# Token-block order for the last two column blocks of a residual projection, and router bookkeeping moved into the first expert pair, in a mixed attention and mixture-of-experts block on one Trainium2 core

## The chip, the cores and the metric

The kernel runs on 1 core of one Trainium2 chip. The metric is the device time in microseconds (us) from the start to the end of one execution. Lower is better. The engines are called PE (matrix multiply), DVE (vector), ACT (scalar activation), POOL (GpSimd) and SP (the queue that issues most DMA transfers).

## What is computed

One layer for 512 tokens of width 1024, all in 32-bit floating point: a merged recurrent and forgetting-attention part, a cross attention over 256 memory rows, and then a mixture of 32 experts of which each token takes two. The change lies between the last product of the cross attention and the first two experts:

```python
x = x + _cross_attention(...)              # its last step is  o @ w_xo,  w_xo is 1024 x 1024
t = _rmsnorm(x, g_moe)
g_logits = t @ w_rg + b_rg                 # 4 groups
e_logits = t @ w_re + b_re                 # 4 groups of 8 experts
g_idx = argmax(g_logits); top_v, top_i = top_k(e_logits of that group, 2)
top_w = softmax(top_v) * softmax(g_logits)[g_idx]
for e in range(32):
    he = silu(t @ w_gate[e]) * (t @ w_up[e])
    y = y + combine[:, e:e + 1] * (he @ w_down[e])
return _rmsnorm(x + y, g_final)
```

The three matrices of one expert are 2 MB each, 201 MB for all 32.

## The kernel before

**The last projection.** `o @ w_xo` is added to the residual `X1` in four column blocks of 256 columns (c = 0 to 3). The 512 tokens are four token blocks (tb = 0 to 3). A weight block of 512 rows x 256 columns (0.5 MB, tile `wraw`) is loaded on SP by `load_w`, split by ACT into a high part `wh` (L124) and by DVE into the rest `wl` (L125), and used by `Rows.block`: four slices of the contraction, three matmuls each (L102 to L104), so 12 matmuls for one token block and half the contraction. Three `wraw` buffers are used in turn, and a new load waits until the block three before it has been split. Blocks c = 2 and 3 are `rw2` and `rw3`.

**The router.** For each token block the new residual rows are transposed on PE (`turn`, L765, copied out by ACT or DVE as `rsc`), multiplied with the router's weights (`logits`, L780), squared on ACT (`squares`, `rstd`, with a power on POOL), scaled into two half-precision parts `xn16` (`parts`: L797 on ACT, L798 on DVE), and for each pair of token blocks h the two experts are chosen on DVE (`choose`), every token gets a rank within its expert (`place`, a few small matmuls L843), and one-hot matrices `G0` are made. `first` (L896) then gathers on PE the tokens of experts 0 and 1 with 64 matmuls. `numbers` makes the slot-to-token table and what later pairs need (`code`, `R`, `tokf`), and `weights` the weight of each slot (`wsl`).

**The order.** In this section PE, DVE and ACT run exactly in the order in which the program writes their steps, and the string `ROUT` sets it: `a`, `b` are halves of `rw2` by token block, `e` adds `rw2` to the residual, `w` is a token block of `rw3`, `v` splits the second weight block of `rw3`, `t`, `l`, `s`, `r`, `X`, `g` are the router's steps above, `C` chooses, `K` places, `G` gathers. SP and POOL are ordered by the scheduler of the compiler.

**The experts.** They run in 16 pairs. A pair has 16 steps of gate and up matmuls (`gate_up`, L1053), 8 steps of down matmuls of the pair before (L1077), two gathers for the next pair (`stationary`, L1028), and the combination of the pair before into the residual (L1103, L1104). Weights come in pieces of 1 MB, 12 in a pair, through a ring of 14 pieces that `RING` lays out: `m` pieces in a pool, `h` and `l` in the buffers of `wh` and `wl`, `r` in space that is free after the projection. `experts.load(9)` issues the first nine `m` pieces before the router starts.

Of the kernel before, what the change touches and what calls it, by code (L numbers as in the profile page):

```python
# [9 lines left out]
F32 = mybir.dt.float32  # L10
F32R = mybir.dt.float32r
# [9 lines left out]
P = 128  # L21
# [15 lines left out]
CAP = 64  # L37
NPAIR = NE // 2
MAXOV = 16
NRAW = 10  # L40
RING = "m m m m m m m m m h l r r m".split()
NAHEAD = 11


ROUT = ("a0 a1 t00 a2 t01 l00 a3 t02 l01 b0 t03 l02 v b1 l03 b2 b3 e s0 s1 w0 t10 t11 s2 w1 l10 l11 t12 t13 s3 r0 w2 l12 "
        "l13 r1 t20 X0 w3 r2 t21 l20 g0 X1 r3 t22 l21 g1 C0 t23 l22 l23 K0 g2 g3 C1 X2 K1 X3 G0 G1")
NR = 8 + NE

C_MLQ, C_MLK, C_MLV, C_MLO = 0, 512, 1024, 2048
# [8 lines left out]
def emit(ctx, tc, a):  # L58
# [51 lines left out]
    def load_w(src, k0, nk, c0, n):  # L110
        i = wx[0] if wx else -1
        if wx:
            wx[0] += 1
        pool, nb = (wx[1], 3) if i == 0 else (wp, 3)
        raw = pool.tile([P, 1024], F32, name="wraw", tag="wraw", bufs=nb)
        SP.dma_start(raw.rearrange("p (j n) -> p j n", j=nk),
                     src[k0 * P:(k0 + nk) * P, c0:c0 + n].rearrange("(j p) n -> p j n", p=P))
        if i == 2:
            h = wx[1].tile([P, 1024], F32R, name="wh", tag="wraw", bufs=3)
            l = wx[1].tile([P, 1024], F32R, name="wl", tag="wraw", bufs=3)  # L120
        else:
# [537 lines left out]

    mraw = ctx.enter_context(right("mraw"))  # L660
    wx[:] = [0, s_ot.enter_context(left("wx"))]
    router, experts = moe(ctx, tc, a, X1, dram, small, acc, pss, pso, left, right, ident, rpow, wp, rt_, mraw)
    rw2, rw3 = (resid_rows(a["w_xo"], oth, otl, c) for c in (2, 3))
    with tc.manual_schedule(engines={mybir.EngineType.PE, mybir.EngineType.DVE, mybir.EngineType.Activation}):
        rw2.loads()
        rw3.ws = [rw3.load(0)]
        experts.load(9)
        for w in ROUT.split():
            n = [int(x) for x in w[1:]]
            if w[0] in "ab":  # L670
                drain(rw2.block(4 * "ab".index(w[0]), rw2.ws["ab".index(w[0])], n[0]))
            elif w == "e":
                rw2.done()
            elif w == "v":
                rw3.ws.append(rw3.load(4))
                experts.load(NAHEAD)
            elif w[0] == "w":
                drain(rw3.of_block(n[0]))
            else:
                router[w[0]](*n)  # L680
    s_ot.close()
# [44 lines left out]
    return c  # L726


def moe(ctx, tc, a, X2, dram, small, acc, pss, pso, left, right, ident, rpow, wp, c, mraw):
    nc = tc.nc  # L730
    V, S, G, TE, SP = nc.vector, nc.scalar, nc.gpsimd, nc.tensor, nc.sync
    rc, iot, Eb, Ab, rk, tokf, wsl = c.pool, c.iot, c.Eb, c.Ab, c.rk, c.tokf, c.wsl
# [8 lines left out]

    c.hits = hits

    slots, tTs = [], []

    sq, lgs, m8s, ids = {}, {}, {}, {}
    ss = rc.tile([P, NB, 2], F32, name="ss")

    READY = ((0, 4), (4, 6), (6, 8))

    def turned(stage, tb):

        if not tTs:
            tTs.append(mraw.tile([P, 4, 4, P], F32, name="rsc", tag="mw", bufs=NRAW))
        k0, k1 = READY[stage]
        if stage == 0:
            return tTs[0][:, tb]
        return tTs[0][:, 2 * stage - 2 + tb // 2, tb % 2 * 2:tb % 2 * 2 + 2]

    def turn(stage, tb):  # L760
        k0, k1 = READY[stage]
        n = k1 - k0
        pt = pss()
        for j in range(n):
            TE.transpose(pt[:, j * P:(j + 1) * P], X2[tb][:, (k0 + j) * P:(k0 + j + 1) * P], ident)  # L765
        ptv = pt[:, :n * P].rearrange("p (j t) -> p j t", j=n)
        if stage == 2:
            V.tensor_copy(turned(stage, tb), ptv)
        else:
            S.activation(turned(stage, tb), ptv, AF.Copy)  # L770

    lp = []

    def logits(stage, tb):

        if not lp:
            lp.append(pso())
        k0, k1 = READY[stage]
        for k in range(k0, k1):
            TE.matmul(lp[0][:, tb * NR:(tb + 1) * NR], turned(stage, tb)[:, k - k0], c.wr[:, k],  # L780
                      start=k == 0 and tb == 0, stop=k == KB - 1 and tb == NB - 1, skip_group_check=True)

    def squares(tb, cs=slice(0, 6 * P), i=0):
        S.activation(c.XN[:, 0, tb, cs].bitcast(BF), X2[tb][:, cs], AF.Square, accum_out=ss[:, tb, i:i + 1])

    def rstd(tb):
        squares(tb, slice(6 * P, D), 1)
        v = small.tile([P, 1], F32, name="vv", tag="vv")
        V.tensor_scalar(v, ss[:, tb, 0:1], ss[:, tb, 1:2], D * EPS, op0=OP.add, op1=OP.add)
        V.tensor_scalar(v, v, 1.0 / (D * XS * XS), None, op0=OP.mult)  # L790
        sq[tb] = rpow(v)
# [62 lines left out]
        for tb in (2 * h, 2 * h + 1):  # L854
            hits(c.G0, c.GA, cd[:, tb % 2], tb)

    def numbers(h):

        bs = slice(2 * h, 2 * h + 2)

        jk = rc.tile([P, 2, 2, NE], F32, name="jk", tag="jk", bufs=1)
        rf = small.tile([P, 2, 2], F32, name="rf", tag="rf")
        V.tensor_scalar(rf, rk[:, bs], -FAR, None, op0=OP.add)
        V.tensor_mul(jk, Eb[:, bs], rf[:, :, :, None].to_broadcast([P, 2, 2, NE]))
        V.scalar_tensor_tensor(c.code[:, bs], jk[:, :, 0], FAR, jk[:, :, 1], op0=OP.add, op1=OP.add)
# [22 lines left out]
    def first(h):  # L888

        if not c.pts:  # L890
            c.pts += [pss(), pss()]
        for g, pt in enumerate(c.pts):
            for i in range(4):
                for j in range(4):
                    tb, k = 2 * h + i // 2, 4 * g + j
                    TE.matmul(pt[:, j * P:(j + 1) * P], c.XN[:, i % 2, tb, k * P:(k + 1) * P], c.G0[:, tb],  # L896
                              start=h + i + j == 0, stop=h == 1 and i + j == 6, skip_group_check=True)

    router = dict(G=first, X=parts, C=choose, K=place, t=turn, l=logits, s=squares, r=rstd, g=scaled)
    c.numbers = numbers  # L900
    experts = Experts(ctx, tc, a, X2, dram, small, acc, pss, pso, left, right, ident, rpow, wp, c, mraw)
    return router, experts

# [1 line left out]
class Experts:  # L905
# [29 lines left out]
    def piece(self, src, w, h, kind):  # L935

        r, n = ((4, DE), (4, DE), (2, D))[w]
        src = src[:, h * r:(h + 1) * r]
        if kind in "mr":
            pool, nb = (self.mraw, NRAW) if kind == "m" else (self.mr2, 2)  # L940
# [25 lines left out]
def run_experts(ex, ctx, tc, a, X2, dram, small, acc, pss, pso, left, right, ident, rpow, wp, c, mraw):  # L966
# [5 lines left out]
    gfin = sg.tile([P, D], F32, name="gfin")  # L972
    G.dma_start(gfin, a["g_final"].to_broadcast([P, D]))

    def weights():

        wpt = c.wparts
        dn = sg.tile([P, NB], F32, name="dn")
# [6 lines left out]
        V.tensor_copy(wpt[:, :, :, 1], rem)  # L985
        V.tensor_sub(rem, rem, wpt[:, :, :, 1])
        V.tensor_copy(wpt[:, :, :, 2], rem)
        pw = pss()
        for tb in range(NB):
            for j in range(2):  # L990
                Vw = sg.tile([P, 3, NE], BF, name="Vw", tag="Vw", bufs=1)
                V.tensor_mul(Vw, Eb[:, tb, j][:, None, :].to_broadcast([P, 3, NE]),
                             wpt[:, tb, j, :, None].to_broadcast([P, 3, NE]))
                TE.matmul(pw[:, :3 * NE], c.R[:, tb, j], Vw.rearrange("p a e -> p (a e)"),
                          start=tb + j == 0, stop=tb + j == NB)
        pwv = pw[:, :3 * NE].rearrange("p (v a b) -> p v a b", v=3, b=2)
        for h in range(2):
            r = slice(h * 64, h * 64 + 64)
# [290 lines left out]
```

## Time and profile before

| | |
|---|---|
| median of 3 runs | 1309.62 us (1306.95 to 1310.33) |
| the profiled execution | 1310.08 us, its span 1308.3 us |
| PE busy | 1253.9 us, 96% of the span |
| DVE, ACT, POOL busy | 42%, 27%, 10% |
| moved by DMA | 278.45 MB, mean 213 GB/s |
| chain that ended last | PE 92%, DVE 4%, ACT 1% |

Times in the trace are counted from the span's start. The projections before the section of the change end near 748 us, the router runs to 806 us, and the sixteen expert pairs follow.

### The profile page before, as it was taken

How to read it: one execution, taken by the hardware profiler on the slowest of the kernel's cores; microseconds unless marked ns; L12 is line 12 of the kernel's file. 1: busy time of each engine (PE TensorE's matmuls, PEld its weight loads, DVE VectorE, ACT ScalarE, POOL GpSimd, SP SyncE). 2: the span in 40 equal slices, each digit the busy share in tenths (PEclk: the TensorE clock that was granted, in tenths of full speed). 3: DMA queues.
4: the chain of work that ended last, by engine and by line, in shares of the span. 5: the costliest groups of instructions: out<-in, count | busy, mean ns of one | idle time of the engine just before them, and what ended most of it. 6: DMA issues, size and time to landing. Idle time of an engine off the chain costs nothing.

```text
span 1308.3 us, 18639 instructions
## 1 busy us (share of the span) xinstructions
PE 1253.9 (96%) x7606; PEld 899.9 (69%) x7606; DVE 552.9 (42%) x1054; ACT 355.4 (27%) x627; POOL 130.0 (10%) x250
## 2 busy tenths in 40 slices
PE   6999999999999999999999985999999999999996
PEld 5898999888888977899977983444444444444443
DVE  4436455334566654447555435132323322222225
ACT  4435344222344433235434351000000000000102
POOL 0001011000001010001000003111111211111001
PEclk9999999999999999999999996899999999999998
DMA  4342432344254325234521553999999999999971
GB/s 166 86 109 84 79 95 72 92 97 92 86 89 81 89 87 155 91 119 138 186 70 62 209 211 124 361 409 417 417 416 416 419 417 416 414 418 417 418 324 66
DMA packets 99113, 278.45 MB, mean 213 GB/s; under 512 B 6196, under 2 KB 67908, under 8 KB 77904
## 3 DMA queue, kind: packets, MB, share of 16 engines
q1 hardware_dynamic: 97536, 272.46, 58.1%
q0 software_dynamic: 1488, 4.76, 1.1%
q8 instruction: 61, 1.00, 0.3%
q14 instruction: 28, 0.23, 0.1%
HBM read 275.08 MB, written 2.12 MB: 212 GB/s over the span
## 4 chain that ended last, share of the span: by engine, by line
PE 92%; DVE 4%; ACT 1%; issue 1%; DMA 1%; POOL 0%; SPq 0%; POOLq 0%; ACTq 0%; DVEq 0%
PE acc L1053 18%; PE acc L102 16%; PE acc L104 16%; PE acc L103 16%; PE pso L1077 8%; PE pss L1028 4%; PE pss L1103 1%; PE pso L1103 1%; PE pso L1104 1%; PE pss L102 1%; PE pss L104 1%; PE pss L103 1%; PE pss L1066 1%; PE pss L1104 1%; DVE st L1030 1%
## 5 line engine op out<-in xcount | busy, mean ns | idle before, releaser
L1053 PE MATMUL acc<-mw,st 128*64 128x512 f32 x880 | 239.5, 608 | 0.0
L125 DVE TENSOR_TENSOR wl<-wraw,wh 128x1024 fp32r<-128x1024 f32 x120 | 146.9, 1225 | 193.0 <-ACT wh L124 188.5
L124 ACT ACTIVATE wh<-wraw 128x1024 fp32r<-128x1024 f32 x120 | 126.9, 1059 | 195.2 <-PE acc L103 92.5
L1053 PEld LDWEIGHTS acc<-mw,st 128*64 128x64 f32 x880 | 68.1, 139 | 111.1 <-issue 106.9
L102 PE MATMUL acc<-hH,wh 128*128 128x512 f32 x320 | 128.5, 401 | 0.0
L103 PE MATMUL acc<-hL,wh 128*128 128x512 f32 x320 | 127.7, 399 | 0.0
L104 PE MATMUL acc<-hH,wl 128*128 128x512 f32 x320 | 125.9, 401 | 1.7 <-DVE wl L125 1.7
L1088 DVE SCALAR_TENSOR_TENSOR yl<-pso,wsl,yh 128x512 fp32r<-128x512 f32 x32 | 22.6, 747 | 225.4 <-ACT yh L1087 225.4
L1077 PE MATMUL pso<-mw,hT 128*64 128x512 f32 x440 | 112.6, 592 | 0.7 <-ACT hT L1068 0.7
L103 PE MATMUL acc<-wl,hH 128*128 128x256 f32 x384 | 109.3, 285 | 1.1 <-DVE wl L125 1.1
L102 PE MATMUL acc<-wh,hH 128*128 128x256 f32 x384 | 109.4, 286 | 0.8 <-ACT wh L124 0.8
L104 PE MATMUL acc<-wh,hL 128*128 128x256 f32 x384 | 109.1, 285 | 0.2 <-DVE hL L196 0.2
L1039 POOL TENSOR_SCALAR G<-iot,code 128x64 f16<-128x64 f32 x120 | 50.7, 449 | 342.5 <-PE pss L1028 322.9
L1077 PEld LDWEIGHTS pso<-mw,hT 128*64 128x64 f32 x440 | 37.2, 137 | 61.4 <-issue 59.7
L103 PEld LDWEIGHTS acc<-wl,hH 128*128 128x128 f32 x384 | 73.1, 191 | 1.9 <-DVE wl L125 1.5
L102 PEld LDWEIGHTS acc<-wh,hH 128*128 128x128 f32 x384 | 72.8, 190 | 1.7 <-ACT wh L124 1.2
L104 PEld LDWEIGHTS acc<-wh,hL 128*128 128x128 f32 x384 | 73.3, 191 | 0.5 <-DVE hL L196 0.4
L104 PEld LDWEIGHTS acc<-hH,wl 128*128 128x128 f32 x320 | 60.6, 189 | 16.0 <-DVE wl L125 2.2
L1028 PEld LDWEIGHTS <-xn 128*128 128x128 f16 x960 | 55.3, 99 | 23.2 <-issue 22.7
L103 PEld LDWEIGHTS acc<-hL,wh 128*128 128x128 f32 x320 | 60.7, 190 | 13.4
L102 PEld LDWEIGHTS acc<-hH,wh 128*128 128x128 f32 x320 | 60.6, 189 | 13.3 <-ACT wh L124 0.4
L1087 ACT ACTIVATE yh<-pso,wsl 128x512 fp32r<-128x512 f32 x32 | 20.3, 684 | 154.1 <-PE pso L1077 154.1
(321 smaller groups left out, 2341.0 us busy)
## 6 DMA issues: line engine op xcount, KB each, us to landing
mw<-w_gate SPq DMA_DIRECT2D x55, 1024.0 KB, 12.7
mw<-w_up SPq DMA_DIRECT2D x55, 1024.0 KB, 11.7
mw<-w_down SPq DMA_DIRECT2D x55, 1024.0 KB, 10.1
wraw<-w_in SPq DMA_DIRECT2D x64, 512.0 KB, 5.5
wraw<-w_xkv SPq DMA_DIRECT2D x16, 512.0 KB, 3.4
mwl<-w_gate SPq DMA_DIRECT2D x10, 512.0 KB, 8.7
mwh<-w_up SPq DMA_DIRECT2D x10, 512.0 KB, 8.9
mwh<-w_down SPq DMA_DIRECT2D x10, 512.0 KB, 11.1
```

The source lines that it names most:

```text
L102: TE.matmul(out, ah, bh, start=start, stop=False, **kw)
L103: TE.matmul(out, ah, bl, start=False, stop=False, **kw)
L104: TE.matmul(out, al, bh, start=False, stop=stop, **kw)
L124: S.activation(h, raw, AF.Copy)
L125: V.tensor_sub(l, raw, h.bitcast(F32))
L1028: TE.matmul(pt[:, j * n:(j + 1) * n], c.XN[:, i % 2, i // 2, (4 * g + j) * P:(4 * g + j + 1) * P], G_[:, i // 2, :n], start=i == 0, stop=i ...
L1039: G.tensor_scalar(G_[:, tb, i * 64:i * 64 + 64], iot[:, :64], c.code[:, tb, e:e + 1], None, op0=OP.is_equal)
L1053: TE.matmul(ps[i][half(h)], sts[k // 4][:, k % 4, half(h)], w[i][k], start=k == 0, stop=k == KB - 1)
L1077: TE.matmul(o[n][half(h)], hT[:, j, half(h)], w[j][:, n * 512:(n + 1) * 512], start=j == 0, stop=j == 3)
L1088: V.scalar_tensor_tensor(yl[:k, c], o[n][:k], wcol, yh[:k, c].bitcast(F32), op0=OP.mult, op1=OP.subtract)
L1103: TE.matmul(o, C[:k, ts], yh[:k, c], start=True, stop=False)
L1104: TE.matmul(o, C[:k, ts], yl[:k, c], start=False, stop=True)
```

## The change

Both `rw2` and `rw3` are now done whole by token block (`x` and `p` in `ROUT`), each token block is added to the residual at once, and the router's steps of token blocks 0 and 1 come between. The transposes have two stages of 512 columns in place of three of 512, 256 and 256. The split parts of the two weight blocks of `rw2` have buffers of their own, while all four `wraw` blocks share the three common buffers. `v` comes first. The slot numbers and weights are taken out of the stretch ahead of the first pair and put behind its sixth step. The ring still has 14 pieces, with nine `m` and three `r`.

```diff
-NRAW = 10
-RING = "m m m m m m m m m h l r r m".split()
+NRAW = 9
+NTAIL = 3
+RING = "m m m m m m m m m h l r r r".split()
-ROUT = ("a0 a1 t00 a2 t01 l00 a3 t02 l01 b0 t03 l02 v b1 l03 b2 b3 e s0 s1 w0 t10 t11 s2 w1 l10 l11 t12 t13 s3 r0 w2 l12 "
-        "l13 r1 t20 X0 w3 r2 t21 l20 g0 X1 r3 t22 l21 g1 C0 t23 l22 l23 K0 g2 g3 C1 X2 K1 X3 G0 G1")
+ROUT = ("v x0 t00 t01 s0 l00 p0 t02 l01 t03 s1 r0 x1 l02 t10 X0 l03 p1 l10 r1 s2 x2 t11 X1 s3 g0 l11 g1 C0 p2 r2 x3 t12 "
+        "X2 K0 l12 g2 p3 t13 r3 l13 g3 C1 G0 K1 X3 G1")
...
-        pool, nb = (wx[1], 3) if i == 0 else (wp, 3)
-        raw = pool.tile([P, 1024], F32, name="wraw", tag="wraw", bufs=nb)
+        raw = wp.tile([P, 1024], F32, name="wraw", tag="wraw", bufs=3)
...
-        if i == 2:
-            h = wx[1].tile([P, 1024], F32R, name="wh", tag="wraw", bufs=3)
-            l = wx[1].tile([P, 1024], F32R, name="wl", tag="wraw", bufs=3)
+        if i in (0, 1):
+            h = wx[1].tile([P, 1024], F32R, name="wh", tag="wx", bufs=4)
+            l = wx[1].tile([P, 1024], F32R, name="wl", tag="wx", bufs=4)
...
-            if w[0] in "ab":
-                drain(rw2.block(4 * "ab".index(w[0]), rw2.ws["ab".index(w[0])], n[0]))
-            elif w == "e":
-                rw2.done()
-            elif w == "v":
+            if w == "v":
                 rw3.ws.append(rw3.load(4))
                 experts.load(NAHEAD)
-            elif w[0] == "w":
-                drain(rw3.of_block(n[0]))
+            elif w[0] in "xp":
+                drain((rw2 if w[0] == "x" else rw3).of_block(n[0]))
...
-    READY = ((0, 4), (4, 6), (6, 8))
+    READY = ((0, 4), (4, 8))
...
-    def numbers(h):
+    def codes(h):
...
+    def numbers(h):
...
         if not c.pts:
             c.pts += [pss(), pss()]
-        for g, pt in enumerate(c.pts):
-            for i in range(4):
+        for i in range(4):
+            for g, pt in enumerate(c.pts):
...
-    def weights():
+    Vw = sg.tile([P, 2 * NB, 3, NE], BF, name="Vw")
+
+    def weight_parts():
...
+        V.tensor_mul(Vw, Eb.rearrange("p b j e -> p (b j) e")[:, :, None, :].to_broadcast([P, 2 * NB, 3, NE]),
+                     wpt.rearrange("p b j a -> p (b j) a")[:, :, :, None].to_broadcast([P, 2 * NB, 3, NE]))
+
+    def weights():
+
         pw = pss()
-        for tb in range(NB):
-            for j in range(2):
-                Vw = sg.tile([P, 3, NE], BF, name="Vw", tag="Vw", bufs=1)
-                V.tensor_mul(Vw, Eb[:, tb, j][:, None, :].to_broadcast([P, 3, NE]),
-                             wpt[:, tb, j, :, None].to_broadcast([P, 3, NE]))
-                TE.matmul(pw[:, :3 * NE], c.R[:, tb, j], Vw.rearrange("p a e -> p (a e)"),
-                          start=tb + j == 0, stop=tb + j == NB)
+        for i in range(2 * NB):
+            TE.matmul(pw[:, :3 * NE], c.R[:, i // 2, i % 2], Vw[:, i].rearrange("p a e -> p (a e)"),
+                      start=i == 0, stop=i == 2 * NB - 1)
...
-            for h in range(2):
-                c.numbers(h)
...
+            if p == 0:
+                advance(gu, 6)
+                with tc.manual_schedule(engines={mybir.EngineType.DVE, mybir.EngineType.Activation}):
+                    for f in (c.codes, c.numbers):
+                        for h in range(2):
+                            f(h)
+                    weight_parts()
...
-            advance(gu, 4)
+            advance(gu, 4 if p else 2)
...
-            advance(gu, 4)
+            advance(gu, 4 if p else 0)
```

**On SP, at the end of the projection.** `wraw` are weight blocks of `w_xo`, `mw` the first nine pieces of expert weights, `mwl` the first piece that goes into the buffers of `wl`. Before:

```order
L116 DMA wraw_7209<-w_xo 128x4x256
L116 DMA wraw_7215<-w_xo 128x4x256
L116 DMA wraw_7337<-w_xo 128x4x256
L942 DMA mw_7221<-w_gate 128x2048
L942 DMA mw_7223<-w_up 128x2048
L942 DMA mw_7225<-w_gate 128x2048
L942 DMA mw_7227<-w_up 128x2048
L942 DMA mw_7229<-w_up 128x2048
L942 DMA mw_7231<-w_gate 128x2048
L942 DMA mw_7233<-w_up 128x2048
L942 DMA mw_7235<-w_gate 128x2048
L942 DMA mw_7237<-w_gate 128x2048
```

And now:

```order
L116 DMA wraw_7215<-w_xo 128x4x256
L931 DMA mw_7221<-w_gate 128x2048
L931 DMA mw_7223<-w_up 128x2048
L931 DMA mw_7225<-w_gate 128x2048
L931 DMA mw_7227<-w_up 128x2048
L931 DMA mw_7229<-w_up 128x2048
L931 DMA mw_7231<-w_gate 128x2048
L931 DMA mw_7233<-w_up 128x2048
L931 DMA mw_7235<-w_gate 128x2048
L931 DMA mw_7237<-w_gate 128x2048
L116 DMA wraw_7239<-w_xo 128x4x256
L936 DMA mwl_7249<-w_gate 128x1024
```

The second weight block of `rw3` (7337 before, 7239 now) has moved from ahead of the nine pieces to behind them. The first block of `rw2` (7203) has moved too: before it was issued during the `w_xkv` loads, now it stands three places ahead of the pieces.

**On ACT, at the same place.** `wh` are the high parts of the weight blocks, `rsc` the transposed residual, `xn16,ss` the squares. Before:

```order
L124 ACTIVATE wh_7205<-wraw_7203 128x1024
L124 ACTIVATE wh_7211<-wraw_7209 128x1024
L124 ACTIVATE wh_7217<-wraw_7215 128x1024
L770 ACTIVATE rsc_7268<-pss_7263 128x512
L770 ACTIVATE rsc_7268<-pss_7282 128x512
L770 ACTIVATE rsc_7268<-pss_7305 128x512
L770 ACTIVATE rsc_7268<-pss_7327 128x512
L124 ACTIVATE wh_7339<-wraw_7337 128x1024
```

And now:

```order
L124 ACTIVATE wh_7205<-wraw_7203 128x1024
L124 ACTIVATE wh_7211<-wraw_7209 128x1024
L124 ACTIVATE wh_7217<-wraw_7215 128x1024
L124 ACTIVATE wh_7241<-wraw_7239 128x1024
L757 ACTIVATE rsc_7283<-pss_7278 128x512
L757 ACTIVATE rsc_7290<-pss_7285 128x512
L770 ACTIVATE xn16_7195,ss_7196<-x1_4532 128x512
L757 ACTIVATE rsc_7328<-pss_7323 128x512
```

The split of the second weight block of `rw3` now stands ahead of the first copy of a transpose. On DVE its other half (`wl_7242`) stands in the same way ahead of the first addition of `rw2` to the residual.

**On DVE, at the end of the router.** `GA` and `G0` are the one-hot matrices that `first` needs, `code`, `R` and `Vj` belong to the slot numbers, `st` is the scaled gather with which the first pair starts. These rows follow the ranks of the second pair of token blocks now:

```order
L849 TENSOR_TENSOR jk_8184<-eb_5658,rf_8185 128x128
L734 TENSOR_SCALAR GA_5667<-iot_5647,cd_7688 128x128
L850 SCALAR_TENSOR_TENSOR code_5665<-jk_8184 128x64
L856 TENSOR_TENSOR R_5661<-iot64_5649,rk_5660 128x512
L862 TENSOR_SCALAR Vj_8189<-eb_5658,tokn_5651 128x64
L735 SCALAR_TENSOR_TENSOR G0_5666<-iot_5647,cd_7688,GA_5667 128x128
L734 TENSOR_SCALAR GA_5667<-iot_5647,cd_7688 128x128
L862 TENSOR_SCALAR Vj_8189<-eb_5658,tokn_5651 128x64
L856 TENSOR_TENSOR R_5661<-iot64_5649,rk_5660 128x512
L735 SCALAR_TENSOR_TENSOR G0_5666<-iot_5647,cd_7688,GA_5667 128x128
L784 SCALAR_TENSOR_TENSOR xn16_7195<-x1_4532,rpow_7613,xn16_7195 128x1024
L1022 TENSOR_TENSOR st_8158<-pss_7643,gsc_5640 128x512
```

Though the program writes them behind the sixth step of the first pair, `code`, `R` and half of `Vj` stand on DVE still ahead of `st`, between the one-hot matrices. Only the other half of `Vj`, `tokf` and the weights come after `st`.

## Rows read from the trace of the kernel before

**Rows 1.** Busy time by stretch: length, PE, PEld, DVE, ACT, POOL, granted clock, DMA share, GB/s.
```profile
750.00:800.00 50.00, 37.51 (x325) 36.17 (x324) 26.55 (x95) 22.69 (x47) 2.79 (x5) 0.86 0.56 211
1000.00:1100.00 100.00, 99.22 (x606) 45.01 (x604) 29.52 (x46) 8.13 (x14) 14.58 (x27) 1.00 1.01 417
```

**Rows 2.** Timeline of PE: the same instruction in two successive expert pairs (start, duration).
```profile
867.50 0.75 PE L1066 MATMUL pss<-ident,ul 128*128 128x128 f32 x4
897.68 0.75 PE L1066 MATMUL pss<-ident,ul 128*128 128x128 f32 x4
```

**Rows 3.** Timeline of PE: end of the router and the first expert pair.
```profile
794.28 0.18 PE L843 MATMUL pso<-ab,before 128*128 128x32 bf16 x1 [5.34 <-DVE ab L834]
...
806.25 13.43 PE L1053 MATMUL acc<-mw,st 128*64 128x512 f32 x48
...
823.59 3.61 PE L1028 MATMUL pss<-G,xn 128*128 128x128 f16 x32
827.13 4.66 PE L1053 MATMUL acc<-mw,st 128*64 128x512 f32 x16
...
833.62 0.64 PE L1053 MATMUL acc<-mw,st 128*64 128x512 f32 x1
```

**Rows 4.** Busy time by 2 us stretches (columns as in rows 1).
```profile
806.00:808.00 2.00, 2.00 (x8) 0.73 (x9) 0.40 (x3) 0.00 (x0) 2.00 (x6) 0.50 0.04 8
...
812.00:814.00 2.00, 2.00 (x12) 0.63 (x10) 0.00 (x0) 0.00 (x0) 2.00 (x2) 0.97 0.24 45
...
824.00:826.00 2.00, 2.00 (x22) 2.00 (x20) 0.85 (x5) 0.00 (x0) 0.00 (x0) 0.50 1.01 422
```

**Rows 5.** SP's timeline; time to landing of issues at 736.01, 736.98, 739.90, and of all.
```profile
736.98 0.42 SPq L942 DMA_DIRECT2D mw<-w_up  x1
...
739.90 2.57 SPq L942 DMA_DIRECT2D mw<-w_gate  x2
...
wraw<-w_xo SPq DMA_DIRECT2D x1, 512.0 KB, 3.4
mw<-w_up SPq DMA_DIRECT2D x1, 1024.0 KB, 7.6
mw<-w_gate SPq DMA_DIRECT2D x1, 1024.0 KB, 21.1
...
mw<-w_gate SPq DMA_DIRECT2D x55, 1024.0 KB, 12.7
```

**Rows 6.** Timelines of PE, ACT, DVE: 24 projection matmuls from 747.84, transposes, logits, copy, splits.
```profile
747.84 0.28 PE L102 MATMUL acc<-wh,oth 128*128 128x256 f32 x1
...
750.66 0.60 PE L765 MATMUL pss<-ident,x 128*128 128x128 f32 x4
...
752.96 0.98 PE L780 MATMUL pso<-wr,rsc 128*128 128x40 f32 x8
...
751.29 0.60 ACT L770 ACTIVATE rsc<-pss 128x512 f32<-128x512 f32 x1 [1.24 <-PE pss L765]
...
759.15 1.05 ACT L124 ACTIVATE wh<-wraw 128x1024 fp32r<-128x1024 f32 x1
...
760.24 1.23 DVE L125 TENSOR_TENSOR wl<-wraw,wh 128x1024 fp32r<-128x1024 f32 x1 [8.74 <-ACT wh L124]
```

**Rows 7.** Timelines of ACT and DVE: `parts`, and first and last step of `choose` and `place`.
```profile
781.25 2.15 ACT L797 ACTIVATE xn<-x,rpow 128x1024 f16<-128x1024 f32 x1 [0.52 <-POOL rpow L98]
...
783.71 0.29 DVE L813 MAX8 m<-lg 128x8 f32<-128x8 f32 x2
...
786.61 0.19 DVE L834 TENSOR_TENSOR ab<-eb 128x64 bf16<-128x64 bf16 x1
788.38 0.29 DVE L846 TENSOR_TENSOR jk<-eb,pso 128x128 f32<-128x128 bf16 x1 [1.25 <-PE pso L843]
...
790.53 0.35 DVE L739 SCALAR_TENSOR_TENSOR G<-iot,cd,GA 128x128 f16<-128x128 f32 x1
...
798.60 2.05 DVE L798 SCALAR_TENSOR_TENSOR xn<-x,rpow,xn 128x1024 f16<-128x1024 f32 x1
```

More of the change, by code (lines that the diff above doesn't have):

```diff
@@ L661, in emit @@
     wx[:] = [0, s_ot.enter_context(left("wx"))]
-    router, experts = moe(ctx, tc, a, X1, dram, small, acc, pss, pso, left, right, ident, rpow, wp, rt_, mraw)
+    router, experts = moe(ctx, tc, a, X1, dram, small, acc, pss, pso, left, right, ident, rpow, wp, rt_, mraw, wx[1])
     rw2, rw3 = (resid_rows(a["w_xo"], oth, otl, c) for c in (2, 3))
@@ L726, in router_consts, with moe @@
     return c
-def moe(ctx, tc, a, X2, dram, small, acc, pss, pso, left, right, ident, rpow, wp, c, mraw):
+def moe(ctx, tc, a, X2, dram, small, acc, pss, pso, left, right, ident, rpow, wp, c, mraw, wx):
     nc = tc.nc
@@ L742, in moe @@
     c.hits = hits
-    slots, tTs = [], []
+    slots, tTs = [], {}
     sq, lgs, m8s, ids = {}, {}, {}, {}
     ss = rc.tile([P, NB, 2], F32, name="ss")
-    READY = ((0, 4), (4, 6), (6, 8))
[L751 to L758, printed above, removed]
+    READY = ((0, 4), (4, 8))
     def turn(stage, tb):
-        k0, k1 = READY[stage]
-        n = k1 - k0
         pt = pss()
[L764 to L768, printed above, removed]
+        for j, k in enumerate(range(*READY[stage])):
+            TE.transpose(pt[:, j * P:(j + 1) * P], X2[tb][:, k * P:(k + 1) * P], ident)
+        t = tTs[stage, tb] = wx.tile([P, 4, P], F32, name="rsc", tag="rsc", bufs=2)
+        ptv = pt.rearrange("p (j t) -> p j t", j=4)
+        if (stage, tb) == (1, NB - 1):
+            V.tensor_copy(t, ptv)
         else:
-            S.activation(turned(stage, tb), ptv, AF.Copy)
+            S.activation(t, ptv, AF.Copy)
     lp = []
@@ L777, in logits, with squares @@
             lp.append(pso())
-        k0, k1 = READY[stage]
-        for k in range(k0, k1):
-            TE.matmul(lp[0][:, tb * NR:(tb + 1) * NR], turned(stage, tb)[:, k - k0], c.wr[:, k],
+        for j, k in enumerate(range(*READY[stage])):
+            TE.matmul(lp[0][:, tb * NR:(tb + 1) * NR], tTs[stage, tb][:, j], c.wr[:, k],
                       start=k == 0 and tb == 0, stop=k == KB - 1 and tb == NB - 1, skip_group_check=True)
-    def squares(tb, cs=slice(0, 6 * P), i=0):
+    def squares(tb, cs=slice(0, D // 2), i=0):
         S.activation(c.XN[:, 0, tb, cs].bitcast(BF), X2[tb][:, cs], AF.Square, accum_out=ss[:, tb, i:i + 1])
     def rstd(tb):
-        squares(tb, slice(6 * P, D), 1)
+        squares(tb, slice(D // 2, D), 1)
         v = small.tile([P, 1], F32, name="vv", tag="vv")
@@ L865, in numbers @@
         V.scalar_tensor_tensor(c.code[:, bs], jk[:, :, 0], FAR, jk[:, :, 1], op0=OP.add, op1=OP.add)
+    def numbers(h):
+        bs = slice(2 * h, 2 * h + 2)
         Vj = rc.tile([P, 2, 2, NE], F16, name="Vj", tag="Vj", bufs=1)
@@ L899, in moe @@
     router = dict(G=first, X=parts, C=choose, K=place, t=turn, l=logits, s=squares, r=rstd, g=scaled)
-    c.numbers = numbers
+    c.codes, c.numbers = codes, numbers
     experts = Experts(ctx, tc, a, X2, dram, small, acc, pss, pso, left, right, ident, rpow, wp, c, mraw)
@@ L939, in piece @@
         if kind in "mr":
-            pool, nb = (self.mraw, NRAW) if kind == "m" else (self.mr2, 2)
+            pool, nb = (self.mraw, NRAW) if kind == "m" else (self.mr2, NTAIL)
             t = pool.tile([P, r, n], F32, name="mw", tag="mw", bufs=nb)
```

## The prediction, made before the changed kernel was run

> **What bounds the kernel now.** I read the stretches first, then PE's timeline, then who it waits for, then the transfers. In the expert pairs PE is busy 99.22 of 100 us and the DMA engines are full at 417 GB/s [rows 1]. One pair takes 897.68 - 867.50 = 30.18 us [rows 2], and its 12 pieces of 1.049 MB at 417 GB/s take as long. Both are full, but PE sets the pace: a piece is issued when PE has freed its buffer, lands 12.7 us later in the median [rows 5], and the ring of 14 pieces in steps of 12 leaves it some 30 us until its use. So the pairs behind the first only shift, and what counts is when the second pair starts: at 833.62 us [rows 3]. The slack is ahead of that. From 750 to 800 us PE is busy 37.51 of 50 us [rows 1]. It waits 5.34 us for the choice of the experts on DVE [rows 3], starts the first pair at 806.25, and runs its first six microseconds, and a gather near 824, at half the granted clock (0.50, the lower of the two levels, 1.2 GHz) [rows 3, 4].
>
> **Unit prices.** The 24 projection matmuls of two half token blocks took 750.66 - 747.84 = 2.82 us, which is what a whole token block takes now [rows 6]. The row of four logits matmuls has 0.98 and that of four transposes 0.60; less the part in which the next instruction already runs I take 0.8 and 0.4 (estimates) [rows 6]. A copy of a transpose is 0.60, a split of a weight block 1.05 on ACT and 1.23 on DVE [rows 6]. `parts` is 2.15 on ACT and 2.05 on DVE, `choose` 786.80 - 783.71 = 3.1, the vector part of `place` 790.88 - 788.38 = 2.5 [rows 7]. Twelve steps of the first pair took 13.43 with 5.8 us of them at half clock, which cost 2.9, so a step at full clock is 0.87 [rows 3, 4].
>
> **Term 1, a weight block that comes late: +15 us.** The second weight block of `rw3` used to be issued at 736 us, ahead of the nine expert pieces. Now it stands behind them on SP. It must wait for two things there, the split of the block whose buffer it takes and its turn, and then for the 9.4 MB in front; the last of the three is the longest. The pieces land in the order of their issue: the second, issued at 736.98, 7.6 us later at 744.6; the eighth, issued at 739.90, 21.1 us later at 761.0. That is 16.4 us for six, 2.7 each [rows 5]. So the ninth lands near 763.7 and half a megabyte behind it 1.4 later, at 765. PE cannot go round it. It does the first token block of `rw2` (747.84 + 2.82 = 750.7) and two transposes (751.5), and then needs the first copy of a transpose, which stands on ACT behind the split of the late block. The split ends at 766.1, the copy at 766.7, and PE has been idle for 15.2 us. DVE stands still as well, at its half of the split, so nothing behind is done in advance. Before, the same block was split at 759 with everything else running [rows 6].
>
> **Term 2, the clock after it: +2.4 us.** When the first pair began after a thin stretch, the granted clock was 0.50 until about 812, 5.8 us into solid work [rows 4]. After an idle stretch of 15 us I take 5 us of work at that level. Bounds: nothing, and the 2.9 of the first pair.
>
> **Term 3, the router's chain from there to the first pair.** From 766.7 PE does the logits and transposes of both stages and `p0`, `x1`, `p1`, `x2`, up to the transpose `t11`: four token blocks 11.3, five logits 4.0, four transposes 1.6, small gaps 0.3: together 17.2, and with term 2 it is at 786.3. From then on DVE and ACT set the pace in turn: the copy 0.6, `parts` of token block 1 2.15 and 2.05, two scalings 0.4, `choose` 3.1, gaps 0.2: 794.8. Then, queued in order on DVE, the addition of `p2`, its squares and power (some 2.2 in all), the addition of `x3` (0.4), `parts` 2.15 and 2.05, `place` 2.5, and the addition of `p3` (0.6 with a scaling), which PE had finished near 800: 804.7. Then the last transpose and its copy 1.1, logits at half clock 1.6, scaling 0.2, `choose` 3.1, the rank matmuls 0.5, `place` 2.5, the slot-number steps that DVE now runs between (`code`, `R`, half of `Vj`: 2.6 as I add them up from rows of their kind, bounds 0 and 4), `parts` 2.05, eight gathers and the scaling 1.8, gaps 0.2: the first pair starts near 820.3, against 806.25. That is +14.0. Had the block come in time, the same sum would start near 751.8 rather than 766.7, without term 2: 820.3 - 14.9 - 2.4 = 803.0, or -3.2. So weaving alone brings 3 us here: the 5.34 us wait is spread, but DVE has the same two choices and more copies to add in one queue.
>
> **Term 4, the first pair: -5 us.** Before, it ran from 806.25 to 833.62, 27.4 us [rows 3]. The weights took PE from 819.68 to 823.59, 3.9 us for eight small matmuls that each had to wait for a DVE product in a single buffer [rows 3]. With all products in one instruction they take about 0.5: -3.4. The clock fell in that gap and was 0.50 at 824 to 826 [rows 4]; the gather of 3.61 and four steps of 4.66 [rows 3] would take about 1.9 and 3.5 at full clock: -2.9. The eight slot-number matmuls come in, +0.4, and the start is bounded by the second `st`, +0.7. Sum -5.2: 22.2 us, from 820.3 to 842.5. The half clock at the start stays, since PE is thin before it as before.
>
> **Sum.** The second pair starts at 842.5 instead of 833.62: +8.9, and the rest follows unchanged. The ring's pieces that wait for the end of the projection (five, 12.6 us at 417 GB/s) are issued near 800 and land near 815, well ahead of the second pair, so I cost them at nothing; without that cover it would be up to 5 more. The profiled execution took 1310.08, which is 0.46 above the median; 1310.08 + 8.9 = 1319.0 in such a run, 1318.5 in the median. My sum takes every chain at its longest, so I take **1318**.
>
> **The rivals.** *The block overtakes the pieces.* If the half megabyte does not have to wait for the nine pieces, it lands 3.4 us after its issue at 744.6, where the queue has room (as the block at 736.01 did [rows 5]), at 748.0, and there is no idle stretch: terms 1 and 2 vanish, -3.2 - 5.2 = -8.4, 1301.2 in the median. It decides below a landing of about 757. Against it stands the spacing of the landings, 2.7 us a piece in the order of issue. I give it 0.12. The Trainium skill (DMA: Bandwidth & Descriptors, section Queues, rings and completion order) says that a later transfer may finish its write before an earlier one, since data descriptors carry no barrier, though each DMA engine takes its descriptors in ring order. By the first clause this rival would be possible; the trace of before shows no landing out of order. *The stall is real but dear parts go.* If the clock does not fall (-2.4 and -2.9 at the first pair's start) and the block lands 1 us earlier, the sum is +2.6: 1312.2, within 0.3% (3.9 us, about what a measurement of this kernel can tell from no change). 0.13. *The stream of weights becomes the bound.* The ring starts to drain 14 us later relative to its filling, and if the pieces that now come late meet the second pair, up to 5 us are added: 1323. Against it, they have some 27 us. 0.07. The forecast itself has 0.68.
>
> **The numbers.** Slower by over 0.3%: 0.68 + 0.07 = 0.75. Within: 0.13. Faster: 0.12. The forecast's own range, from a landing 2 us earlier and no slot-number steps in the chain (-5) to 3 us more in the chain, is 1313 to 1321. To leave out no more than 0.2 I go down to 1308, which takes in the second rival, and up to 1323 for the third.
>
> **What would show it.** Right: the late `w_xo` block issued after the ninth piece and landing near 765; PE idle some 15 us from 751.5, released by ACT's copy; the granted clock at 0.50 after it; the first pair at about 820 and the second at 842; no row of PE waits for weight products. Wrong: PE busy through 752 to 765, or a first pair that starts before 810; or PE waits for DMA in the second pair.

## The result, and the profile after

The changed kernel took 1321.88 us in the median of 4 runs (1318.45 to 1323.66), the kernel before 1308.98 beside it. The ratio is 1.0097, 95% interval 1.0069 to 1.0124: slower, by 12.9 us. The profiled execution of the change is its shortest: 1318.45 us, span 1316.7, where [rows 1 to 7] come from an execution of the kernel before that took 1310.08, span 1308.3. Between these two the loss is 8.4 us; what makes other executions longer is shown below. Of all executions reported here one, of the kernel that issues the late block ahead of all pieces, took 1795.02 us at a mean granted clock of 0.655, against 0.988 to 0.991 in its other seven, and is left out of that kernel's ratio.

The same two stretches as in [rows 1], with the same columns:

```profile
750.00:800.00 50.00, 30.14 (x214) 29.70 (x213) 12.01 (x37) 14.56 (x31) 1.27 (x3) 0.76 0.25 102
1000.00:1100.00 100.00, 99.22 (x588) 43.38 (x586) 26.14 (x41) 8.64 (x14) 14.55 (x27) 1.00 1.01 417
```

The expert pairs are as before. From 750 to 800 us PE works 7.4 us less than before, at a lower clock. Who PE waited for from 740 us to the end (total us, times, longest):

```profile
PE pso L766 <- ACT rsc L757: 15.4, 2, 14.8
PE pso L766 <- DVE lg L790: 5.0, 1, 5.0
...
PE pss L885 <- DVE G L735: 3.2, 1, 3.2
PE pss L751 <- DVE x L525: 3.0, 1, 3.0
```

PE's timeline gives the place of each, and the first pair, which answers to [rows 3]:

```profile
750.27 1.03 PE L751 MATMUL pss<-ident,x 128*128 128x128 f32 x8
766.11 1.93 PE L766 MATMUL pso<-wr,rsc 128*128 128x40 f32 x8 [14.81 <-ACT rsc L757]
...
785.31 0.60 PE L751 MATMUL pss<-ident,x 128*128 128x128 f32 x4
790.95 1.90 PE L766 MATMUL pso<-wr,rsc 128*128 128x40 f32 x8 [5.05 <-DVE lg L790]
...
809.25 0.44 PE L751 MATMUL pss<-ident,x 128*128 128x128 f32 x2 [2.99 <-DVE x L525]
...
818.48 2.72 PE L885 MATMUL pss<-G,xn 128*128 128x128 f16 x24 [3.22 <-DVE G L735]
...
822.90 5.37 PE L1045 MATMUL acc<-mw,st 128*64 128x512 f32 x24 [0.56 <-DVE st L1022]
...
834.39 0.51 PE L986 MATMUL pss<-Vw,R 128*128 128x96 bf16 x8
...
842.09 0.64 PE L1045 MATMUL acc<-mw,st 128*64 128x512 f32 x1
```

The first pair starts at 822.90 (before 806.25) and takes 19.2 us (before 27.4); the second starts at 842.09 (before 833.62), 8.5 us later, which is the loss of the span. Nothing is lost or won behind it.

The timelines of SP, ACT and DVE show what PE waited for:

```profile
740.38 2.93 SPq L931 DMA_DIRECT2D mw<-w_gate  x2
745.52 0.38 SPq L116 DMA_DIRECT2D wraw<-w_xo  x1
...
764.52 1.06 ACT L124 ACTIVATE wh<-wraw 128x1024 fp32r<-128x1024 f32 x1 [21.49 <-DMA wraw<-w_xo]
765.48 1.06 ACT L757 ACTIVATE rsc<-pss 128x512 f32<-128x512 f32 x2
...
788.58 2.05 DVE L784 SCALAR_TENSOR_TENSOR xn<-x,rpow,xn 128x1024 f16<-128x1024 f32 x1 [2.66 <-ACT xn L783]
790.55 0.26 DVE L790 SCALAR_TENSOR_TENSOR lg<-pso,rpow,br 128x40 f32<-128x40 f32 x1
792.89 0.26 DVE L790 SCALAR_TENSOR_TENSOR lg<-pso,rpow,br 128x40 f32<-128x40 f32 x1 [2.09 <-PE pso L766]
```

The weight block is issued behind the ninth piece and lands 19 us later; ACT had waited 21.49 us for it, and only then copies the transposes. The second wait is another thing. `l11`, the logits of token block 1's second half, writes into the PSUM tile that `g0` reads for token block 0. In `ROUT` `g0` stands ahead of `l11`, and on DVE it stands behind the second step of `X1` (`xl`, the lower of the two half-precision parts, 2.05 us). So PE, ready at 785.9, waits for a read of another slice of the same tile: token block 0's columns, where `l11` writes those of token block 1. The kernel before had waits of this kind already, two of them, in the trace that the prediction was made from:

```profile
PE pso L780 <- DVE lg L804: 3.0, 2, 1.9
```

The granted clock behind both waits, by 2 us (columns as in [rows 1]; it is third from the end):

```profile
768.00:770.00 2.00, 2.00 (x11) 2.00 (x11) 0.00 (x0) 0.00 (x0) 0.00 (x0) 0.50 0.00 0
770.00:772.00 2.00, 2.00 (x17) 2.00 (x17) 0.00 (x0) 0.00 (x0) 0.00 (x0) 0.88 0.00 0
772.00:774.00 2.00, 2.00 (x20) 2.00 (x19) 0.42 (x1) 0.69 (x2) 0.00 (x0) 1.00 0.00 0
...
792.00:794.00 2.00, 2.00 (x10) 2.00 (x11) 1.04 (x9) 0.00 (x0) 0.00 (x0) 0.50 0.00 0
794.00:796.00 2.00, 2.00 (x12) 2.00 (x10) 1.76 (x13) 1.10 (x7) 0.00 (x0) 0.50 0.00 0
796.00:798.00 2.00, 2.00 (x12) 2.00 (x12) 0.17 (x1) 0.35 (x3) 0.00 (x0) 0.56 0.00 0
```

Each wait is paid a second time, in matmuls at half speed: some 4 us of them behind the first, 6 to 7 behind the second.

### The profile page after: what moved, and what is told of

The parts are those of the page before. It is cut to its first block, busy times and chain, and to the rows that moved or that the text cites. A ratio compares the mean times of both kernels' runs of the same rounds, so it can differ in the third digit from the quotient of the medians.

```text
span 1316.7 us, 18633 instructions
## 1 busy us (share of the span) xinstructions
PE 1252.7 (95%) x7606; PEld 902.3 (69%) x7606; DVE 553.1 (42%) x1046; ACT 355.1 (27%) x626; POOL 131.9 (10%) x250
## 4 chain that ended last, share of the span: by engine, by line
PE 90%; DVE 3%; DMA 3%; ACT 1%; issue 1%; SPq 0%; POOL 0%; POOLq 0%; ACTq 0%; DVEq 0%
PE acc L1045 17%; PE acc L103 16%; PE acc L105 16%; PE acc L104 16%; PE pso L1069 8%; PE pss L1020 4%; DMA wraw<-w_xo 1%; PE pss L1095 1%; PE pso L1096 1%; PE pso L1095 1%; PE pss L103 1%; PE pss L105 1%; PE pss L104 1%; PE pss L1058 1%; PE pss L1096 1%
## 5 line engine op out<-in xcount | busy, mean ns | idle before, releaser
L1045 PE MATMUL acc<-mw,st 128*64 128x512 f32 x880 | 235.8, 598 | 0.6 <-DVE st L1022 0.6
L1080 DVE SCALAR_TENSOR_TENSOR yl<-pso,wsl,yh 128x512 fp32r<-128x512 f32 x32 | 22.6, 746 | 225.3 <-ACT yh L1079 225.3
## 6 DMA issues: line engine op xcount, KB each, us to landing
mw<-w_gate SPq DMA_DIRECT2D x55, 1024.0 KB, 14.4
```

The source lines that it names most:

```text
L1045: TE.matmul(ps[i][half(h)], sts[k // 4][:, k % 4, half(h)], w[i][k], start=k == 0, stop=k == KB - 1)
L1080: V.scalar_tensor_tensor(yl[:k, c], o[n][:k], wcol, yh[:k, c].bitcast(F32), op0=OP.mult, op1=OP.subtract)
```

## The experiments

None of these kernels changes what is computed.

**The changed kernel again**, as the control of the first group (no edit).

> The changed kernel once more, beside the others of this group. Both theories expect its ratio to the kernel before again at 1.007 to 1.012. What it is for: the first profile of it showed the first expert pair's start at 822.9 us with the clock granted in full from there, and one stretch at half clock behind the wait for the router's lg tile (790.7 to 797.5 us). If where the clock falls is what makes its executions differ, this profile shows another set of stretches at half clock and a span that differs by about half their length; if the stretches are the same, the spread comes from elsewhere.

Measured: 1321.02 us (1317.65 to 1323.44), ratio 1.0093, interval 1.0076 to 1.0110. Its profiled execution took 1323.44 us; it is called the long execution below, and that of the first profile, 1318.45, the short one. PE's timeline:

```profile
825.66 7.59 PE L1045 MATMUL acc<-mw,st 128*64 128x512 f32 x24 [0.36 <-DVE st L1022]
...
834.06 5.37 PE L1045 MATMUL acc<-mw,st 128*64 128x512 f32 x24
```

Its second pair starts at 847.07, 5.0 us behind the first profile's, as its span is 5.0 longer. The two long waits are the same (14.78 and 5.0 us). Of the 5.0 us of difference 0.9 were there before the section began, 1.9 came between the stall and the first pair, and 2.2 in the pair. The clock was lower in each thin stretch: 0.50 in place of 0.63 at 766 to 772 us, 0.50 in place of 0.57 at 790 to 798, 0.70 in place of 0.81 at 806 to 824. At the first pair it shows best. Busy time from 822 to 834 us, first in the short execution, then in this one:

```profile
822.00:834.00 12.00, 11.11 (x63) 3.84 (x60) 5.35 (x15) 0.00 (x0) 7.46 (x13) 1.00 0.57 194
```

```profile
822.00:834.00 12.00, 10.78 (x57) 4.80 (x54) 3.89 (x6) 0.00 (x0) 6.93 (x13) 0.66 0.19 55
```

In the short execution the clock is back at its upper level, 2.4 GHz, when the pair starts; in the long one it stays at 0.50 until about 830, and the same 24 matmuls take 7.59 in place of 5.37. The Trainium skill (TensorE: Matmul & The Clock Gate, Part 1 on the HAM clock gate) warns that how many slow matmuls one kernel shows changes from run to run; these two profiles agree. So one profile of this kernel says its time to about 5 us only.

**The late block, moved in four steps.** The load that ends the changed kernel's SP queue is issued ahead of all nine pieces (the edit shown), or behind three or six of them (3 or 6 in `load`); PE, DVE and ACT keep their orders. The edit also makes SP follow the program's order in this section, which changes the order of some later pieces; no run has this part alone, with the block left behind nine.

```diff
-    with tc.manual_schedule(engines={mybir.EngineType.PE, mybir.EngineType.DVE, mybir.EngineType.Activation}):
+    with tc.manual_schedule(engines={mybir.EngineType.PE, mybir.EngineType.DVE, mybir.EngineType.Activation,
+                                     mybir.EngineType.SP}):
...
+        experts.load(0)
+        rw3.ws.append(rw3.load(4))
...
-                rw3.ws.append(rw3.load(4))
```

> The changed kernel with the second weight block issued on SP ahead of all nine expert pieces instead of behind them; the orders on PE, DVE and ACT are those of the changed kernel. My theory (the late block is the cost): it lands near 743 us, before its split on ACT and DVE is due, so PE's wait of 14.8 us for the scaled copy and the half clock behind it go. Gain over the changed kernel 14 to 17 us: time about 1305, ratio to the kernel before 0.995 to 0.999, second pair near 826 us. Rival A (the weaving puts too much on DVE, the stall only lets DVE run ahead): without the stall the waits on DVE behind it grow by as much, the gain is under 5 us and the second pair stays behind 836 us. Rival B (the expert pieces, now 1.5 us later each, become the bound): the first pair waits for mw pieces, gain under 10 us.

> The changed kernel with the second weight block issued behind three of the nine expert pieces. Behind six it was split at 756.0 and PE waited 7.2 us, behind nine at 765.4 and 14.8 us; by the same 2.9 us a piece it lands near 747 us, ahead of the first scaled copy. My theory (only what lands after about 749 us costs): no wait of PE over 1 us, clock in full, time as with the block ahead of all nine, 1303 to 1305. Rival (the cost rises with each piece ahead of it, by 1.6 to 2 us): 1308 to 1310.

> The same with the second weight block issued behind six of the nine expert pieces. My theory: the queue lands in order, one piece each 2 to 2.7 us, so the block lands some 6 to 8 us sooner than behind nine, near 757 us, and PE's wait is 7 to 9 us instead of 14.8: gain over the changed kernel 6 to 8 us (7 to 10 if the clock falls later too), time about 1311. Rival (the wait is not for the block but for DVE or ACT): same as the changed kernel, or same as with the block ahead of all.

| pieces ahead | split starts, after the split before it | PE's wait | median us | ratio, interval |
|---|---|---|---|---|
| 0 | 5.6 | 0.25 | 1303.62 | 0.9968 (0.9955 to 0.9980) |
| 3 | 6.2 | 0.25 | 1303.89 | 0.9964 (0.9951 to 0.9977) |
| 6 | 15.0 | 7.24 | 1314.89 | 1.0048 (1.0030 to 1.0066) |
| 9 | 22.6 | 14.81 | 1321.88 | 1.0097 (1.0069 to 1.0124) |

ACT's two splits of each, with three ahead:

```profile
743.05 1.06 ACT L124 ACTIVATE wh<-wraw 128x1024 fp32r<-128x1024 f32 x1 [3.54 <-PE acc L105]
749.27 1.06 ACT L124 ACTIVATE wh<-wraw 128x1024 fp32r<-128x1024 f32 x1 [5.16 <-DMA wraw<-w_xo]
```

and with six:

```profile
741.02 1.06 ACT L124 ACTIVATE wh<-wraw 128x1024 fp32r<-128x1024 f32 x1 [3.54 <-PE acc L105]
756.00 1.06 ACT L124 ACTIVATE wh<-wraw 128x1024 fp32r<-128x1024 f32 x1 [13.92 <-DMA wraw<-w_xo]
```

From six to nine the split comes 22.6 - 15.0 = 7.6 us later, 2.5 a piece, which is what 1.049 MB take at 417 GB/s. With three the block lands just in time and costs nothing that these medians show; without a piece ahead of it, the split waits for PE and not for the load. With the block in front of all, PE's timeline has no stall, and the next wait is the other one, which stands in the same way (5.04 us) with three:

```profile
751.60 1.08 PE L768 MATMUL pso<-wr,rsc 128*128 128x40 f32 x8 [0.25 <-ACT rsc L759]
...
774.48 1.90 PE L768 MATMUL pso<-wr,rsc 128*128 128x40 f32 x8 [5.04 <-DVE lg L792]
...
806.46 5.37 PE L1047 MATMUL acc<-mw,st 128*64 128x512 f32 x24 [0.56 <-DVE st L1024]
...
825.65 0.64 PE L1047 MATMUL acc<-mw,st 128*64 128x512 f32 x1
```

The gain from nine to none is 1321.02 - 1303.62 = 17.4 us in the same group: 14.5 of wait, and the rest, 2.9, is about what half speed over the matmuls behind the stall costs (Term 2). Both rivals of the expectation fall: nothing of the stall was taken up further on, and the pieces, each later, are waited for by nobody. My figure for six pieces, 1311, was too low in the median: four of its six runs took 1315, and two took 1309.8 and 1309.9. The profiled one is of the two, and ran the first 24 matmuls of its first pair in 5.37 us, at the full clock.

**`l11` ahead of `g0`.**

```diff
-... r1 s2 x2 t11 X1 s3 g0 l11 g1 C0 p2 ...
+... r1 s2 x2 t11 X1 s3 l11 g0 g1 C0 p2 ...
```

> The changed kernel with one pair of the router's steps the other way round: the logits of the second half of token block 1 (l11) ahead of the first hit step g0, which shares their PSUM tile, where the changed kernel has them behind it. My theory: PE's wait of 5.05 us for DVE's read of lg goes, the sum of column block C0 ends 2 us sooner and with the DVE work behind it the first pair starts 3 to 5 us sooner: time 1314 to 1316 where the changed kernel's profile had 1318.5, ratio 1.004 to 1.007. Rival (DVE is the bound of that stretch and PE only waits for it elsewhere): the 5 us turn up at the next wait, t13 or the last hit step, and the gain is under 1.5 us.

> Both edits together: the second weight block ahead of the nine expert pieces, and l11 ahead of g0. My theory (two waits in a row on PE's path, independent of each other): the gain of the second over the early block alone is the same 4 to 6 us as it was over the changed kernel, so 1298 to 1300 us where the early block alone had 1303.6; ratio to the kernel before 0.992 to 0.995, below it. Rival (with the block in time DVE is the bound of the router, and the 5 us turn up at the next wait): under 1.5 us, ratio 0.995 to 0.998.

Alone: 1315.05 us, ratio 1.0055 (1.0041 to 1.0069). With the block ahead of all: 1298.12 us, ratio 0.9930 (0.9917 to 0.9942). By the ratios the swap is worth 0.0038, 5.0 us, with the stall and without it: as far as the intervals tell (some 2.5 us on each of these differences) the two waits are independent. Taking both away gives back 21 us, more than the change lost. PE's timeline of the swap alone:

```profile
767.06 1.93 PE L766 MATMUL pso<-wr,rsc 128*128 128x40 f32 x8 [14.89 <-ACT rsc L757]
...
787.79 1.08 PE L766 MATMUL pso<-wr,rsc 128*128 128x40 f32 x8 [0.69 <-ACT rsc L757]
...
795.85 0.44 PE L751 MATMUL pss<-ident,x 128*128 128x128 f32 x2 [0.96 <-DVE x L525]
...
805.14 0.44 PE L751 MATMUL pss<-ident,x 128*128 128x128 f32 x2 [3.86 <-DVE x L525]
...
819.87 6.99 PE L1045 MATMUL acc<-mw,st 128*64 128x512 f32 x24 [0.36 <-DVE st L1022]
```

Of the 5.05 us some 2.5 turn up again as other waits: 0.69 for the copy of `t11`, 0.96 for `x`, and 3.86 in place of 2.99 at the next wait for `x`. The rest of the gain comes with the clock, which stays at 1.00 from 790 to 802 us, where the changed kernel had 0.57 from 790 to 798. PE's timeline with both edits, where the wait of 5 us is gone and the pair starts 5.1 us sooner than with the early block alone, 0.8 of it because its section began that much sooner:

```profile
796.68 2.31 PE L887 MATMUL pss<-G,xn 128*128 128x128 f16 x24 [3.22 <-DVE G L737]
...
801.31 6.68 PE L1047 MATMUL acc<-mw,st 128*64 128x512 f32 x24 [0.36 <-DVE st L1024]
...
821.81 0.64 PE L1047 MATMUL acc<-mw,st 128*64 128x512 f32 x1
```

**The pair's part alone, and the weaving alone.** The weaving is the new order of `w_xo` and the router in `ROUT`. The first kernel here is the kernel before with the slot numbers, `weight_parts` and one batch of weight products inside the first pair; the second is the changed kernel with these taken back. The edit of the first, without the parts that only divide functions:

```diff
-            for h in range(2):
-                c.numbers(h)
...
+            if p == 0:
+                advance(gu, 6)
+                with tc.manual_schedule(engines={mybir.EngineType.DVE, mybir.EngineType.Activation}):
+                    for f in (c.codes, c.numbers):
+                        for h in range(2):
+                            f(h)
+                    weight_parts()
```

> The kernel before with the pair's part of the change alone: slot numbers and weights inside the first pair, one batch of weight products; w_xo and the router as in the kernel before. My theory: the gaps of 3.6 us for the slots and 4.7 us between weights that PE showed in the pair go, the half clock behind them too, and the slot steps of DVE come ahead of st for some 2 us: gain 4 to 7 us, time 1300 to 1303, ratio 0.995 to 0.997. Rival (the pair is bound by what DVE does ahead of it in any case): the pair starts as much later as it is shorter, same within 1.5 us.

> The changed kernel without the pair's part: w_xo and the router woven, slot numbers and weights where the kernel before has them. My theory (the parts add up): the pair is again 27 us instead of 19 to 22 and its start 0 to 2.6 us sooner, since the slot steps stand behind st again: 3 to 7 us longer than the changed kernel, time 1324 to 1328, ratio 1.012 to 1.017. Rival (in the changed kernel's pair the weights are hidden anyway): within 1.5 us of the changed kernel.

The pair's part alone: 1301.18 us, ratio 0.9952 (0.9937 to 0.9966), as expected. The weaving alone: 1331.39 us, ratio 1.0176 (1.0161 to 1.0190), more than I had expected. PE's timeline of the weaving alone shows why:

```profile
819.22 3.60 PE L882 MATMUL pss<-G,xn 128*128 128x128 f16 x32 [2.00 <-DVE G L735]
825.24 0.35 PE L861 MATMUL acc<-Vj,R 128*128 128x32 f16 x4 [2.42 <-DVE Vj L859]
826.95 0.36 PE L861 MATMUL acc<-Vj,R 128*128 128x32 f16 x4 [1.36 <-DVE Vj L859]
827.24 13.38 PE L1039 MATMUL acc<-mw,st 128*64 128x512 f32 x48
```

Its pair takes 27.3 us as before, but it also starts late: as in the kernel before, between the last gather and the pair PE waits 2.42 and 1.36 us for the slot numbers' operands, with the small matmuls 4.4 us in all. I had counted only DVE's side of that move and expected an earlier start. The pair's part thus saves 6.5 us on the kernel before and some 10 on the woven one.

**The slot-number steps on DVE, and the last `xl`.** Two versions on top of the two edits above (early block, `l11` ahead of `g0`): one block of the order for `st`, the first 24 matmuls and the numbers, so that DVE does `code`, `R` and `Vj` behind `st` (`b_forced`); and the same with `X3` ahead of `l13` and `g3` (`b_all`). The hits in the expectations are the one-hot matrices (`GA`, `G0`), and `ab` is what the rank matmuls read.

```diff
             sts = [stationary(c.G0, g, pt=c.pts[g]) for g in range(2)]
+            ps0 = [acc(), acc()]
+            gu0 = gate_up(sts, [(ex.rows(e, 0), ex.rows(e, 1)) for e in (0, 1)], ps0)
+            advance(gu0, 6)
+            for f in (c.codes, c.numbers):
+                for h in range(2):
+                    f(h)
+            weight_parts()
...
```

```diff
-"X2 K0 l12 g2 p3 t13 r3 l13 g3 C1 G0 K1 X3 G1")
+"X2 K0 l12 g2 p3 t13 r3 X3 l13 g3 C1 G0 K1 G1")
```

> The version before (early block, l11 ahead of g0) with two DVE pieces taken off the way to the first pair: the slot-number steps (code, R, Vj) behind the two st instead of between the hits of the last two token blocks, and the last xl of 2.05 us (X3) ahead of g3 instead of behind the hits. My theory: from the end of C1 to the first st DVE has 3.1 us less of code, R and Vj and 2.05 us less of xl, of which the transposes and the last gather of PE hide some; the first pair starts 3 to 4.5 us sooner and the slots' steps fit under its first 24 matmuls of 5.4 us. Time 1294 to 1297, ratio 0.988 to 0.991. Rival (PE's gathers G1, of 2.7 and 0.6 us, or the steps of ACT are as late as DVE): gain under 1.5 us; or the slot numbers come late and PE waits in the pair for R: the same gain is lost there.

> The early block and l11 ahead of g0, with the slot-number steps of DVE (code, R, Vj) behind the two st, and nothing else. In the run that also moved the last xl the hits of the last two token blocks ended 2.7 us after ab instead of 4.6 us, but its xl came 2 us too late for ACT's xh and pushed the chain back by 3.9 us. My theory: without that move the 1.9 us stay, the first pair starts 1.5 to 2 us sooner and the slots' steps fit under its first 24 matmuls: time 1296 to 1297 where the version without it had 1298.1, ratio 0.991 to 0.992. Rival (st is bound by xl and the last gather, not by the hits; or the clock takes it back): within 0.7 us of 1298.1.

With the slot-number steps and `X3` both moved: 1299.67 us, ratio 0.9938 (0.9926 to 0.9951), no gain; my theory falls for the move of `X3`. DVE's timeline:

```profile
791.76 2.07 DVE L786 SCALAR_TENSOR_TENSOR xn<-x,rpow,xn 128x1024 f16<-128x1024 f32 x1 [2.95 <-ACT xn L785]
793.75 0.25 DVE L792 SCALAR_TENSOR_TENSOR lg<-pso,rpow,br 128x40 f32<-128x40 f32 x1
```

`xl` waits 2.95 us for ACT's `xh`, and `g3`, which was ready, stands behind it: it runs at 793.75 in place of 790.71 in the version that leaves `X3` where it was, and the first pair starts at 803.28 in place of 800.26. What was taken off the end was put back at the start with interest.

The slot-number steps alone: 1296.08 us, ratio 0.9901 (0.9886 to 0.9915), the shortest of all kernels here, 0.99 of the kernel before. DVE's timeline, `ab` and the last hit, first with this edit, then without it:

```profile
793.79 0.19 DVE L822 TENSOR_TENSOR ab<-eb 128x64 bf16<-128x64 bf16 x1
...
796.49 0.35 DVE L737 SCALAR_TENSOR_TENSOR G<-iot,cd,GA 128x128 f16<-128x128 f32 x1
```

```profile
792.93 0.19 DVE L822 TENSOR_TENSOR ab<-eb 128x64 bf16<-128x64 bf16 x1
...
797.56 0.34 DVE L737 SCALAR_TENSOR_TENSOR G<-iot,cd,GA 128x128 f16<-128x128 f32 x1
```

The last hit ends 3.1 us after the start of `ab`, in place of 5.0 without the edit, so these steps held up the hits by 1.9 us. In the profiles the first pair starts at 800.26 in place of 801.31, though its section began 0.6 us later. The two medians are from different groups; their ratios differ by 0.0029, 3.8 us, with an uncertainty of some 2.5, so the size of this gain beyond 1.9 us is not settled.

## Why the prediction was right, and where its steps were off

The forecast was 1318 us and slower; the median was 1321.88, inside the range of 1308 to 1323. It lies above the forecast's own range of 1313 to 1321: only the allowance up to 1323 takes it in, and that was made for the third rival, which did not come. So the number came out within the range in part by luck. The mechanism was right: the late block stalls PE and the clock falls behind it. Term 3 was too small, and Term 4 too large for one kind of execution. In the long execution (the control) the terms read like this, beside those of the short one:

| step | predicted | short | long |
|---|---|---|---|
| Term 1, PE idle for the late block | 15.2 | 14.8 | 14.8 |
| Term 3, from there to the first pair | 53.6 | 56.8 | 58.7 |
| Term 4, the first pair | 22.2 | 19.2 | 21.4 |
| second pair starts | 842.5 | 842.1 | 847.1 |

That the start of the second pair is met to 0.4 us in the short execution is luck: Term 3 was 3.2 us too small there and Term 4 3.0 too large. In the long one Term 3 is 5.1 too small and Term 4 only 0.8 too large.

*Term 1* held: issue behind the ninth piece, split at 764.5 (predicted 765), idle 14.8 us. The rival in which the block overtakes the pieces fell: its landing moves with the number of pieces ahead of it. The Trainium skill (DMA: Bandwidth & Descriptors, section Queues, rings and completion order) says both that each DMA engine takes descriptors in ring order and that later writes may finish first; the four places of the block fit the first, and none of these runs shows the second.

*Term 2*, +2.4, held in size: 17.4 us were gained for 14.5 of wait. In the short execution the clock was 0.50 until about 770, in the long one until about 772.

*Term 3* was mis-sized. The step that failed is "From then on DVE and ACT set the pace in turn" from `t11` to the end of the first choice, put at 794.8. It was 796.2 in the short execution, because the sum had no wait of `l11` for `g0`: it took the chain of data alone, not the shared PSUM tile. PE's 5.05 us idle there were followed by more than 6 us at the lower clock, so `p2` came late too, and "p3 added" at 804.7 became 809.2. The swap gave back 5.0 us, and with it the stretch from the stall to the first pair takes 52.8 us (767.06 to 819.87), 0.8 less than the 53.6 of the sum. The waits could have been in the sum, as the trace of the kernel before had two of 3.0 us in all. The statement that "My sum takes every chain at its longest" was wrong for the same reason. Against it, the last stretch to the first pair was 1.9 us shorter than I had it, part of that the slot-number steps, 1.9 us where I took 2.6.

The side sum "803.0, or -3.2" for a block in time rested on the same omission: with the early block the first pair starts at 806.46, and only with `l11` first at 801.31. Beside the pair's part alone (ratio 0.9952) weaving with the block in time costs some 2 us (0.9968), and without the second wait it brings 3 (0.9930); each of these differences has an uncertainty of some 2.5 us, so the first is not clear of noise and the second barely.

*Term 4* depends on the clock. At full clock the pair is 19.2 us. "The half clock at the start stays" came true in the long execution and not in the short one; weights came at 0.5 as predicted.

*The third rival*, a stream of weights that becomes the bound, is out: no profile of the change shows PE waiting for a piece, though the median landing of `w_gate` rose from 12.7 [rows 5] to 14.4 us. The second rival, a clock that does not fall, came true at the first pair of the short execution alone, where it was worth 2.2 us, and the wait missing in Term 3 covered it.

## What to carry to other kernels

A load that is needed within 15 us must not be queued behind prefetches that are needed 60 us later: here the place in the order of issue decided 17 us, and a place behind three of nine pieces cost nothing that was seen. When steps are woven by hand, list for each one not only whose data it needs but also which reads of its output tile stand ahead of it in another engine's order; here the swap of two names gave 5 us. And before work is moved ahead in a queue, ask what ready work stands behind it and whether its own operand is there: the moved `xl` gave back all that it took away.

## What was not expected of the hardware

Two executions of one program with the same long waits differ by 5 us, and 4.1 of them arise where the granted clock differs: in the stretch of 822 to 834 us it was granted at 1.00 in one and at 0.66 in the other. What decides which of them comes is not settled by these runs.
